# A triangular inverse whose 64-row block is transposed by VectorE instead of TensorE, in a one-core decoder layer

## The chip, the cores and the metric

The kernel runs on one core of one Trainium2 chip, in one launch. A core has five engines that run their own instruction streams and wait for each other on semaphores: TensorE (PE in the profile; PEld is its weight load), VectorE (DVE), ScalarE (ACT), GpSimd (POOL) and SyncE (SP), which here only issues DMAs. The metric is the device time of the launch in microseconds; the median of three runs before the change is 2998.03 us (2996.6 to 2998.27).

## The reference

One layer of a decoder over 2048 tokens of width 1024, in fp32: a gated DeltaNet mixer with 8 heads and a 4-head attention to a memory of 256 rows run side by side, their heads are concatenated and projected, then follow a layer norm, a squared-ReLU MLP of width 4096 and a second layer norm.

```python
proj = x @ w_in                              # q, k, v, z, a, b and the memory's queries
q, k, v = silu(causal_conv4(qkv)); q, k = l2_normalize(q), l2_normalize(k)
a_mat = eye + strict_lower(k_beta @ k.T * decay)     # per head and chunk
u = triangular_solve(a_mat, v_beta); w = triangular_solve(a_mat, k_beta * exp(gc))
# scan over chunks: v_new = u - w @ S; o = q_decay @ S + attn @ v_new; S = S * decay + k_decay.T @ v_new
m = memory_attention(mq, mem_k, mem_v)
x = layer_norm(ALPHA * x + concat(o, m) @ w_out)
x = layer_norm(ALPHA * x + square(relu(x @ w_ff1)) @ w_ff2)
```

## The kernel before, in words

The 2048 tokens are worked on in four blocks of 512. In each block the kernel projects head by head (`dense`, line 673), prepares the head's decay matrices and inverts its triangular matrices (`gdn_a`, 818, which calls `invert`, 732), carries the state through the block's four chunks of 128 tokens (`gdn_b`, 869), does the memory attention and the output projection, and then the MLP. Large products are done as three fp32r matmuls on a high and a low part of each operand: ScalarE casts the high part and VectorE subtracts it to get the low part (`split`). Weights come as 128x1024 tiles `wraw` and are split into `whl`.

`invert` is called 32 times, once for each head and block, for four 128x128 unit lower triangular matrices together (the chunks, `c` in `range(NC)`). It builds the inverse from small blocks up. Blocks of 16 are solved on VectorE. Then each doubling, to 32, 64 and 128, takes two small TensorE products of the same form: `pq`, the off-diagonal block of `L` times a known inverse block, which ScalarE copies to `Q`, and `pp`, another known inverse block times `Q`, which goes with a minus sign into the result. The result `Y` is kept transposed, since the next products want it as weights. The left factor of `pp` is needed the other way round: `X32` for the step to 64 (two VectorE copies out of `Z`, the 32-blocks that VectorE has transposed), and `X64` for the step to 128. Before the change `X64` is made by TensorE: four 64x64 transposes `px` of `Y`'s first 64 rows and columns (line 799), and one VectorE copy from PSUM to SBUF (line 802). All these small products are in plain fp32, which takes two passes for a matmul; a transpose takes one.

The MLP's second product is done in four groups of seven block products (`ff_seven`, 991; the table `SEVEN`, 987). Products 1 to 4 of the table take sums of weight blocks. Those sums are made in the first block by VectorE from `wq` tiles (`keep_sums`, 971), written to DRAM (`tsc`) and read back as `wraw`; the other products read `w_ff2` itself.

The order of the work is not the order of the code. All operations go through a recorder, which gives each a cost and then places them by a list schedule (`cost`, 184, and `issue`, 220): an engine that is free takes the ready operation that comes first in the code, with fixed delays between engines and a limited number of buffers for each tag. The outcome is one fixed order for each engine, and each engine works through its order strictly, waiting where an operand is late. So an edit in one place moves instructions on every engine after it.

Every recorded instruction shows line 320 in the profile; groups are told apart by the names of their tiles.

Of the kernel before, what the change touches and what calls it, by code (L numbers as in the profile page):

```python
# [14 lines left out]
P = 128  # L15
# [321 lines left out]
def hybrid_layer(  # L337
# [31 lines left out]
    cst = ctx.enter_context(tc.tile_pool(name="cst", bufs=1))  # L369
    wp = ctx.enter_context(tc.tile_pool(name="wp", bufs=1))  # L370
    tp = ctx.enter_context(tc.tile_pool(name="tp", bufs=1))
    pad = ctx.enter_context(tc.tile_pool(name="pad", bufs=1))
    nc.vector.memset(pad.tile([P, 112], F32, name="shift"), 0.0)
    sp = ctx.enter_context(tc.tile_pool(name="sp", bufs=1))
    sm = ctx.enter_context(tc.tile_pool(name="sm", bufs=1))
    ps = ctx.enter_context(tc.tile_pool(name="ps", bufs=1, space=bass.MemoryType.PSUM))
# [296 lines left out]
    def dense(b, h, T, G, w0=None):  # L673
        res = {}
        for nm, o in (("q", QO), ("k", KO), ("v", VO), ("z", ZO)):
            w = w0 if w0 and nm == "q" else load_in(b, o // P + h)
            a = bank("a" + nm, "acc")
            project(a, w, T)
            c = slot("c" + nm, "d")
            th = slot("th", "th")  # L680
            if nm == "z":
                nc.scalar.activation(th, a, AF.Tanh, scale=0.5)
                nc.vector.scalar_tensor_tensor(out=c, in0=th, scalar=1.0, in1=a, op0=ALU.add, op1=ALU.mult)
            else:
                gi = o // P + h
                raw = rec.buf(tp, (P, TB + 3), F32, "raw", 2, "raw")
                nc.scalar.copy(out=raw[:, 3:], in_=a)
                nc.gpsimd.tensor_copy(raw[:, 0:3], halo[:, gi].part(gi))
                if b < NB - 1:
                    nc.gpsimd.tensor_copy(halo[:, gi].part(gi), raw[:, TB:TB + 3])  # L690
                nc.scalar.activation(c, a, AF.Copy, scale=cw[:, 72 + gi:73 + gi])
                for j in range(3):
                    nc.vector.scalar_tensor_tensor(out=c, in0=raw[:, j:j + TB], scalar=cw[:, j * 24 + gi:j * 24 + gi + 1],
                                                   in1=c, op0=ALU.mult, op1=ALU.add)
                nc.scalar.activation(th, c, AF.Tanh, scale=0.5)
                nc.vector.scalar_tensor_tensor(out=c, in0=th, scalar=1.0, in1=c, op0=ALU.add, op1=ALU.mult)
            res[nm] = c
            if nm in "qk":
                if "kq" not in res:
                    res["kq"] = [rec.buf(tp, (P, 2, TB), F32R, "kq%d" % u, 1, "kq") for u in range(2)]  # L700
                i = "kq".index(nm)
                split(c, res["kq"][0][:, i].part(i), res["kq"][1][:, i].part(i), KQE)
        par = "ga%d" % (h % 2)
        ss = small("ss", [P, 2 * NC])
        kd = res["kd"] = slot("kd", "s%d" % (h % 2))
        for n, nm in enumerate("kq"):
            pt = bank("pt" + nm, par)
            for c in range(NC):
                nc.tensor.transpose(pt[:, c * P:(c + 1) * P], res[nm][:, c * P:(c + 1) * P], ident)
            for c in range(NC):  # L710
                j = small("j" + nm, [P, P], 1)
                nc.scalar.activation(j, pt[:, c * P:(c + 1) * P], AF.Square,
                                     accum_out=ss[:, n * NC + c:n * NC + c + 1])
            if nm == "k":
                for c in range(NC):
                    nc.scalar.activation(kd[:, c * P:(c + 1) * P], pt[:, c * P:(c + 1) * P], AF.Copy,
                                         scale=G["ekd"][:, h, c:c + 1])
        nc.gpsimd.tensor_scalar_add(ss, ss, 4 * RMS_EPS)
        rk = small("rk", [P, NC])
        nc.gpsimd.tensor_tensor(out=rk, in0=ss[:, :NC], in1=mhalf, op=ALU.pow)  # L720
        res["e4"] = small("e4", [P, NC], 4)
        nc.gpsimd.tensor_scalar_mul(res["e4"], ss[:, NC:], P * RMS_EPS)
        res["vbs"] = small("vbs", [P, NC])
        nc.gpsimd.tensor_tensor(out=res["vbs"], in0=G["betah"][:, h], in1=rk, op=ALU.mult)
        bh = res["bh"] = small("bh", [P, NC])
        nc.gpsimd.tensor_tensor(out=bh, in0=G["beta"][:, h], in1=rk, op=ALU.mult)
        nc.gpsimd.tensor_tensor(out=bh, in0=bh, in1=rk, op=ALU.mult)
        res["nbe"] = small("nbe", [P, NC], 4)
        nc.gpsimd.tensor_tensor(out=res["nbe"], in0=bh, in1=G["neg"][:, h], op=ALU.mult)
        return res  # L730

    def invert(L, par):
# [47 lines left out]
        nc.vector.transpose(Z.rearrange("p c f -> p (c f)"), ZT.rearrange("p c f -> p (c f)"))  # L780
        for p in range(2):
            nc.vector.tensor_copy(X32[32 * p:32 * p + 32, :, 32 * p:32 * p + 32], Z[64 * p:64 * p + 32])
        for r in quads:
            nc.scalar.copy(out=Y3[r, :, r], in_=ZT[r])
        pq = bank("pq", "ga%d" % par)[:64, :P].rearrange("p (c f) -> p c f", c=NC)
        for c in range(NC):
            nc.tensor.matmul(pq[:, c], L32[:, c], ZT[:, c], start=True, stop=True)
        nc.scalar.copy(out=Q[:64, :, :32], in_=pq)
        pp = bank("pp", "ga%d" % par)[:64, :P].rearrange("p (c f) -> p c f", c=NC)
        for c in range(NC):  # L790
            nc.tensor.matmul(pp[:, c], X32[:, c], Q[:, c, :32], start=True, stop=True)
        for p in range(2):
            nc.vector.tensor_scalar_mul(Y3[64 * p:64 * p + 32, :, 64 * p + 32:64 * p + 64],
                                        pp[32 * p:32 * p + 32], -1.0)

        pq = bank("pq", "ga%d" % par)[:64, :2 * P].rearrange("p (c f) -> p c f", c=NC)
        for c in range(NC):
            nc.tensor.matmul(pq[:, c], L[:, c, :64], Y3[:, c, 64:], start=True, stop=True)
        px = bank("px", "ga%d" % par)[:64, :2 * P].rearrange("p (c f) -> p c f", c=NC)
        for c in range(NC):  # L800
            nc.tensor.transpose(px[:, c], Y3[:64, c, :64], ident[:64, :64])
        nc.vector.tensor_copy(X64[:64], px)
        nc.scalar.copy(out=Q[:64], in_=pq)
        pp = bank("pp", "ga%d" % par)[:64, :2 * P].rearrange("p (c f) -> p c f", c=NC)
        for c in range(NC):
# [165 lines left out]
    def keep_sums(u, j):  # L971

        if j == 0:
            B = [t[:, n * TB:(n + 1) * TB].part(n) for t in (tok_tile("wq"), tok_tile("wq")) for n in range(2)]
        else:
            B = [rec.buf(tp, (P, TB + 3), F32, "raw", 2, "wq")[:, :TB] for _ in range(2)]
            kq = rec.buf(tp, (P, 2, TB), F32, "kq1", 1, "wq")
            B += [kq[:, n].part(n) for n in range(2)]
        for n in range(4):
            nc.sync.dma_start(out=B[n], in_=w_ff2[u + 2 * (n // 2), n % 2][:, j * TB:(j + 1) * TB])  # L980
        for i, o, x, y in ((1, 0, 1, 0), (3, 1, 3, 1), (2, 3, 3, 0), (4, 2, 2, 3)):
            nc.vector.tensor_tensor(out=B[o], in0=B[x], in1=B[y], op=ALU.subtract)
            nc.sync.dma_start(out=tsc[u, i][:, j * TB:(j + 1) * TB].part(j), in_=B[o])
# [7 lines left out]
    def ff_seven(b, ff1_tiles, relu2, add, norm2):  # L991
        Q = 2 * P
        for g in range(NS):
# [45 lines left out]
            if last:  # L1039
                gb = load_bcast(ln2_g, "l2g"), load_bcast(ln2_b, "l2b")  # L1040
            banks = {}
            for n, (xn, wn, bn, on, (th, nh)) in enumerate(SEVEN):
                if not on:
                    banks[bn] = [bank("af2", ("ga%d" % t) if bn == "A" else "pb") for t in range(2)]
                w = [None, None]
# [223 lines left out]
```

## Time and profile before

| what | value |
|---|---|
| median of three runs | 2998.03 us |
| the profiled execution, by its own time | 2999.08 us |
| its span from first to last instruction | 2997.4 us |
| PE busy | 2945.4 us (98%), 15300 matmul passes |
| DVE busy | 2168.6 us (72%) |
| ACT busy | 1520.3 us (51%) |
| POOL busy | 332.4 us (11%) |
| mean granted TensorE clock | 0.995 of full speed |

A matmul's recorded duration runs into the next one's, since matmuls are pipelined: a 128x512 product shows about 0.39 us while the next one starts 0.23 us after it. What a matmul takes of the span is therefore read from start to start in the timeline. In a timeline row, the columns are the start, the duration from the first to the last instruction merged into the row, the engine, the operation with its tiles, the shape and the count; a bracket holds the idle time just before it and what ended it.

### The profile page before, as it was taken

What the parts mean: (1) busy time and instruction counts of PE and PEld (TensorE: products, weight loads), DVE (VectorE), ACT (ScalarE), POOL (GpSimd) and SP (SyncE); (2) the same over time, 40 slices, a digit from 0 to 9 for tenths busy, and PEclk for the clock granted to TensorE, in tenths of its full rate; (3) what the DMA queues carried; (4) which work ended last, traced back from release to release, by engine and by line L of the source; (5) the groups of instructions that cost most, each with busy time, mean ns of one, the idle gap of its engine ahead of it and who ended that gap; (6) DMA issues with size and microseconds to landing.
All of it is one profiled execution on the core that took longest, in us unless ns stands there. A gap on an engine that the chain in (4) does not pass through costs nothing.

```text
span 2997.4 us, 43880 instructions
## 1 busy us (share of the span) xinstructions
PE 2945.4 (98%) x15300; PEld 2428.1 (81%) x15300; DVE 2168.6 (72%) x5537; ACT 1520.3 (51%) x3582; POOL 332.4 (11%) x808
## 2 busy tenths in 40 slices
PE   7999999999999999999999999999999999999998
PEld 6888788888788878888878887888878888788886
DVE  6898977666777787655577887665667787675667
ACT  5676534544355562544445665344554556444443
POOL 1222100000112211000012221000001222000000
PEclk9999999999999999999999999999999999999999
DMA  6765566656733223444473332244446332324443
GB/s 231 253 218 180 196 209 224 200 183 192 268 142 132 106 89 102 145 137 133 151 268 130 121 119 92 87 152 144 145 159 250 126 134 96 99 88 146 143 147 134
DMA packets 127709, 469.85 MB, mean 157 GB/s; under 512 B 14464, under 2 KB 16896, under 8 KB 109056
## 3 DMA queue, kind: packets, MB, share of 16 engines
q1 hardware_dynamic: 126912, 467.00, 46.2%
q8 instruction: 120, 1.97, 0.3%
q14 instruction: 101, 0.83, 0.1%
q10 hardware_dynamic: 576, 0.06, 0.0%
HBM read 402.97 MB, written 64.03 MB: 156 GB/s over the span
## 4 chain that ended last, share of the span: by engine, by line
PE 88%; DVE 8%; ACT 2%; issue 1%; DMA 1%; POOL 0%; POOLq 0%; ACTq 0%; DVEq 0%; SPq 0%
PE af L320 42%; PE ao L320 8%; PE aq L320 6%; PE ak L320 5%; PE az L320 5%; PE av L320 4%; PE amq L320 3%; PE pc L320 3%; PE pp L320 2%; PE pq L320 2%; PE po L320 2%; PE pkq L320 1%; DVE y L320 1%; PE sps L320 1%; DVE ck L320 1%
## 5 line engine op out<-in xcount | busy, mean ns | idle before, releaser
L320 DVE TENSOR_TENSOR whl<-wraw,whl 128x1024 fp32r<-128x1024 f32 (+1 forms) x446 | 538.7, 1216 | 392.8 <-ACT whl L320 386.1
L320 PE MATMUL af<-Thi,whl 128*128 128x512 f32 (+1 forms) x2304 | 655.9, 369 | 6.9 <-DVE whl L320 4.0
L320 ACT CAST whl<-wraw 128x1024 fp32r<-128x1024 f32 (+1 forms) x446 | 466.1, 1045 | 381.8 <-PE af L320 169.0
L320 PEld LDWEIGHTS af<-Thi,whl 128*128 128x128 f32 x2304 | 421.7, 191 | 78.5 <-DVE whl L320 4.8
L320 PE MATMUL af<-whl,xh 128*128 128x512 f32 x1536 | 476.4, 391 | 3.6 <-DVE whl L320 3.6
L320 PE MATMUL af<-Tlo,whl 128*128 128x512 f32 (+1 forms) x1152 | 424.8, 369 | 0.0
L320 PE MATMUL af<-whl,xl 128*128 128x512 f32 x896 | 347.3, 390 | 0.0
L320 PEld LDWEIGHTS af<-whl,xh 128*128 128x128 f32 x1536 | 288.6, 188 | 68.6 <-DVE whl L320 6.7
L320 PE MATMUL ao<-whl,ch 128*128 128x512 f32 x768 | 249.4, 399 | 0.5 <-DVE y L320 0.5
L320 PEld LDWEIGHTS af<-Tlo,whl 128*128 128x128 f32 x1152 | 220.4, 191 | 34.8
L320 ACT ACTIVATE rl<-af 128x512 f32<-128x512 f32 x128 | 76.5, 598 | 271.0 <-PE af L320 269.0
L320 DVE SCALAR_TENSOR_TENSOR y<-y,af 128x512 f32<-128x512 f32 x224 | 151.3, 684 | 84.1 <-PE af L320 82.9
L320 PEld LDWEIGHTS af<-whl,xl 128*128 128x128 f32 x896 | 168.5, 188 | 35.5
L320 POOL TENSOR_SCALAR ve<-mv 128x1 f32<-128x1 f32 x34 | 23.3, 684 | 1528.8 <-DVE mv L320 1528.8
L320 PE MATMUL aq<-Thi,whl 128*128 128x512 f32 x512 | 181.6, 414 | 7.5 <-ACT Thi L320 7.5
L320 PE MATMUL av<-Thi,whl 128*128 128x512 f32 x512 | 173.0, 402 | 0.0
L320 PE MATMUL ak<-Thi,whl 128*128 128x512 f32 x512 | 172.9, 401 | 0.0
L320 PE MATMUL az<-Thi,whl 128*128 128x512 f32 x512 | 170.2, 400 | 0.0
L320 PEld LDWEIGHTS ao<-whl,ch 128*128 128x128 f32 x768 | 142.6, 188 | 27.0 <-DVE y L320 0.7
L320 PE MATMUL ao<-whl,cl 128*128 128x512 f32 x384 | 153.5, 400 | 0.0
L320 PEld LDWEIGHTS aq<-Thi,whl 128*128 128x128 f32 x512 | 94.3, 192 | 21.5 <-ACT Thi L320 7.5
L320 PEld LDWEIGHTS az<-Thi,whl 128*128 128x128 f32 x512 | 95.9, 190 | 18.8 <-DVE whl L320 0.5
(252 smaller groups left out, 5756.3 us busy)
## 6 DMA issues: line engine op xcount, KB each, us to landing
wraw<-in_w_ff_dram SPq DMA_DIRECT2D x224, 512.0 KB, 4.0
whl<-wsc SPq DMA_DIRECT2D x108, 1024.0 KB, 4.8
wraw<-tsc SPq DMA_DIRECT2D x128, 512.0 KB, 3.3
wsc<-whl SPq DMA_DIRECT2D x36, 1024.0 KB, 4.9
wraw<-in_w_out_dram SPq DMA_DIRECT2D x48, 512.0 KB, 4.1
wraw<-in_w_in_dram SPq DMA_DIRECT2D x35, 512.0 KB, 5.8
wq<-in_w_ff_dram SPq DMA_DIRECT2D x64, 256.0 KB, 4.3
tsc<-wq SPq DMA_DIRECT2D x64, 256.0 KB, 3.3
```

Source lines behind the costliest of these rows:

```text
L320: o.fn(*[res(a) for a in o.args], **{k: res(v) for k, v in o.kw.items()})
```

## The change

Three things are changed.

`X64` is now put together from pieces that exist earlier. Its two diagonal 32-blocks are copied by GpSimd out of `Z` (two new copies of 32x128 per call). Its off-diagonal block is the result `pp` of the step to 64, transposed: VectorE transposes the 32 first rows of that PSUM bank in blocks of 32x32 into the buffer of `Lq`, whose contents are no longer needed by then, and writes it with a minus sign into `X64`. The four TensorE transposes and VectorE's copy of `px` are gone. The upper right block of `X64` stays zero from the memset at the start.

The 448-byte tile `shift`, which only moved what is allocated behind it, is gone, and each of the two `raw` buffers is 224 bytes longer. So the second `raw` buffer lies 224 bytes further, the two `kq` buffers 448 bytes further, and all that follows lies where it was.

In the first group of the first block, the product `A12*B21`, which reads `w_ff2` itself, comes second instead of sixth.

```diff
-    pad = ctx.enter_context(tc.tile_pool(name="pad", bufs=1))
-    nc.vector.memset(pad.tile([P, 112], F32, name="shift"), 0.0)
...
-                raw = rec.buf(tp, (P, TB + 3), F32, "raw", 2, "raw")
-                nc.scalar.copy(out=raw[:, 3:], in_=a)
+                raw = rec.buf(tp, (P, TB + 3 + 56), F32, "raw", 2, "raw")
+                nc.scalar.copy(out=raw[:, 3:TB + 3], in_=a)
...
         for p in range(2):
             nc.vector.tensor_copy(X32[32 * p:32 * p + 32, :, 32 * p:32 * p + 32], Z[64 * p:64 * p + 32])
+            nc.gpsimd.tensor_copy(X64[32 * p:32 * p + 32, :, 32 * p:32 * p + 32], Z[32 * p:32 * p + 32])
...
-        pp = bank("pp", "ga%d" % par)[:64, :P].rearrange("p (c f) -> p c f", c=NC)
+        p32 = bank("pp", "ga%d" % par)
+        pp = p32[:64, :P].rearrange("p (c f) -> p c f", c=NC)
         for c in range(NC):
             nc.tensor.matmul(pp[:, c], X32[:, c], Q[:, c, :32], start=True, stop=True)
+        t32 = Lq[:32].rearrange("p f c -> p (f c)")
+        nc.vector.transpose(t32, p32[:32, :P])
         for p in range(2):
             nc.vector.tensor_scalar_mul(Y3[64 * p:64 * p + 32, :, 64 * p + 32:64 * p + 64],
                                         pp[32 * p:32 * p + 32], -1.0)
+        nc.vector.tensor_scalar_mul(X64[32:64, :, :32], t32.rearrange("p (c f) -> p c f", c=NC), -1.0)
...
-        px = bank("px", "ga%d" % par)[:64, :2 * P].rearrange("p (c f) -> p c f", c=NC)
-        for c in range(NC):
-            nc.tensor.transpose(px[:, c], Y3[:64, c, :64], ident[:64, :64])
-        nc.vector.tensor_copy(X64[:64], px)
...
-            B = [rec.buf(tp, (P, TB + 3), F32, "raw", 2, "wq")[:, :TB] for _ in range(2)]
+            B = [rec.buf(tp, (P, TB + 3 + 56), F32, "raw", 2, "wq")[:, :TB] for _ in range(2)]
...
-            for n, (xn, wn, bn, on, (th, nh)) in enumerate(SEVEN):
+            order = [0, 5, 1, 2, 3, 4, 6] if b == 0 and g == 0 else range(7)
+            for n, (xn, wn, bn, on, (th, nh)) in enumerate(SEVEN[i] for i in order):
```

Since the schedule is made anew, instructions move on every engine. Three places matter below.

On PE, the first inversion of the first block, from the product `pp` of the step to 64 (`X_162`, afterwards `X_157`, is the tile X32; `X_160` is the new kernel's X64; `ak` and `av` are the projections that fill the time). Before:

```order
L320 MATMUL pp<-Q,X_162 64x32 x4
L320 MATMUL ak<-Thi,whl 128x512 x2
L320 MATMUL ak<-Tlo,whl 128x512
L320 MATMUL ak<-Thi,whl 128x512
L320 MATMUL av<-Thi,whl 128x512
L320 MATMUL pq<-Y,dl 64x64 x4
L320 MATMUL av<-Tlo,whl 128x512
L320 MATMUL av<-Thi,whl 128x512 x2
L320 MATMUL av<-Tlo,whl 128x512
L320 MATMUL av<-Thi,whl 128x512
L320 MATMUL px<-ident,Y 64x64 x4
L320 MATMUL av<-Thi,whl 128x512
```

The same place in the changed kernel:

```order
L320 MATMUL pp<-Q,X_157 64x32 x4
L320 MATMUL ak<-Thi,whl 128x512 x2
L320 MATMUL ak<-Tlo,whl 128x512
L320 MATMUL ak<-Thi,whl 128x512
L320 MATMUL av<-Thi,whl 128x512
L320 MATMUL av<-Tlo,whl 128x512
L320 MATMUL pq<-Y,dl 64x64 x4
L320 MATMUL av<-Thi,whl 128x512 x2
L320 MATMUL av<-Tlo,whl 128x512
L320 MATMUL av<-Thi,whl 128x512
L320 MATMUL pp<-Q,X_160 64x64 x4
```

The transposes `px` are gone, `pq` stands behind six large matmuls instead of five, and the last `pp` follows `pq` after four large matmuls.

On DVE, the same inversion, between the product `pp` of the step to 64 and the last write to `Y` before `pq` (the `Lq<-dl` copies belong to the next head). Before:

```order
L320 SCALAR_TENSOR_TENSOR cq<-th,cq 128x512
L320 TENSOR_SCALAR Y<-pp 32x4x32
L320 COPY Lq<-dl 32x4x32
L320 TENSOR_SCALAR Y<-pp 32x4x32
L320 COPY Lq<-dl 32x4x32
```

And in the changed kernel:

```order
L320 SCALAR_TENSOR_TENSOR cq<-th,cq 128x512
L320 STREAM_TRANSPOSE Lq<-pp 32x128
L320 TENSOR_SCALAR Y<-pp 32x4x32
L320 TENSOR_SCALAR X_160<-Lq 32x4x32
L320 COPY Lq<-dl 32x4x32
L320 TENSOR_SCALAR Y<-pp 32x4x32
```

Two operations more, the transpose and the write to X64, stand ahead of the second write to `Y`.

On SP, where the first group of the first block's MLP begins (`wraw<-in_w_ff_dram` loads weights of either MLP product, `tsc<-wq` writes the weight sums, `wraw<-tsc` reads them back). Before:

```order
L320 DMA wraw<-in_w_ff_dram 128x1024
L320 DMA wq<-in_w_ff_dram 128x512 x5
L320 DMA wraw<-in_w_ff_dram 128x1024
L320 DMA wraw<-tsc 128x1024
L320 DMA tsc<-wq 128x512 x2
L320 DMA wq<-in_w_ff_dram 128x512
L320 DMA tsc<-wq 128x512 x4
L320 DMA wraw<-tsc 128x1024
```

And in the changed kernel:

```order
L320 DMA wraw<-in_w_ff_dram 128x1024
L320 DMA tsc<-wq 128x512 x2
L320 DMA wq<-in_w_ff_dram 128x512
L320 DMA wraw<-in_w_ff_dram 128x1024
L320 DMA tsc<-wq 128x512 x2
L320 DMA wq<-in_w_ff_dram 128x512
L320 DMA tsc<-wq 128x512 x2
L320 DMA wraw<-tsc 128x1024
```

The first read-back of a sum now stands behind the loads of one more product and behind more of the writes.

## The prediction

> **What bounds the kernel now.** I read the page's engine shares and its chain of waits first.
>
> ```profile
> PE 2945.4 (98%) x15300; PEld 2428.1 (81%) x15300; DVE 2168.6 (72%) x5537; ACT 1520.3 (51%) x3582; POOL 332.4 (11%) x808
> PE 88%; DVE 8%; ACT 2%; issue 1%; DMA 1%; POOL 0%; POOLq 0%; ACTq 0%; DVEq 0%; SPq 0%
> ```
>
> PE is busy for 98% of the span and makes 88% of the chain that ended last. Next I read who PE waited for; the columns are total us, times and the longest wait.
>
> ```profile
> PE af L320 <- DVE whl L320: 7.6, 10, 1.5
> PE aq L320 <- ACT Thi L320: 7.5, 1, 7.5
> PE ptk L320 <- DVE ck L320: 5.7, 4, 2.0
> ...
> PE pp L320 <- ACT Q L320: 1.6, 6, 0.3
> ```
>
> Nothing larger stands in that view. PE hardly waits, and nowhere for `X64`, the tile that the change makes in another way. So the time is the sum of PE's steps, and the question is what the change does to that sum, and whether it makes PE wait where it now does not.
>
> **The transposes.** Here is PE's timeline at the first inversion, the one whose order is shown above.
>
> ```profile
> 113.81 0.65 PE L320 MATMUL pp<-Q,X 128*64 128x32 f32 x8
> 114.39 0.73 PE L320 MATMUL ak<-Thi,whl 128*128 128x512 f32 x2
> ...
> 115.42 0.40 PE L320 MATMUL av<-Thi,whl 128*128 128x512 f32 x1
> 115.75 0.68 PE L320 MATMUL pq<-Y,dl 128*64 128x64 f32 x8
> ...
> 116.69 0.63 PE L320 MATMUL av<-Thi,whl 128*128 128x512 f32 x2
> 117.16 0.40 PE L320 MATMUL av<-Tlo,whl 128*128 128x512 f32 x1
> 117.39 0.39 PE L320 MATMUL av<-Thi,whl 128*128 128x512 f32 x1
> 117.71 0.41 PE L320 MATMUL px<-ident,Y 64*64 64x64 f32 x4
> 118.05 0.50 PE L320 MATMUL av<-Thi,whl 128*128 128x512 f32 x1
> 118.39 0.40 PE L320 MATMUL av<-Tlo,whl 128*128 128x512 f32 x1
> ```
>
> Large matmuls follow each other in 0.23 us (two from 116.69 to 117.16, one to 117.39). Around `px`, one large matmul, the four transposes and one more large matmul take from 117.39 to 118.39, 1.00 us, where the two alone would take 0.46. The four transposes thus cost 0.54 us: their own 0.34, and 0.1 each for going to the small form and back (0.32 and 0.34 instead of 0.23). There are 128 transposes, so 32 such visits:
>
> ```profile
> L320 PE MATMUL px<-ident,Y 64*64 64x64 f32 x128 | 14.3, 224 | 0.0
> L320 DVE COPY X<-px 64x256 f32<-64x256 f32 x32 | 13.3, 416 | 14.8 <-PE px L320 14.4
> L320 DVE TENSOR_SCALAR Y<-pp 32x128 f32<-32x128 f32 x64 | 18.0, 281 | 9.8 <-PE pp L320 8.7
> L320 DVE COPY X<-Z 32x128 f32<-32x128 f32 x64 | 14.2, 221 | 0.9
> L320 DVE STREAM_TRANSPOSE Z<-ZT 128x128 f32<-128x128 f32 x32 | 9.8, 306 | 0.2
> L320 POOL COPY L<-dl 32x128 f32<-32x128 f32 x64 | 31.2, 487 | 24.7 <-PE pq L320 14.9 <-DVE Bc L320 7.5
> ```
>
> 32 x 0.54 = 17.3 us. In some inversions other small products split the four and the cost is higher, so I take **-18 us**, with 14 (the busy time alone) and 20 as the ends.
>
> **The rest of PE's order.** The new schedule puts other small groups elsewhere: some now stand beside each other, others alone. A group that is set among large matmuls costs the two 0.1 us just read. I added up, for both orders, the usual step of each matmul behind its two predecessors as the trace has it, and the changed order comes out about 5 us shorter beyond the transposes, but part of that is short waits that the trace has in such places. I take **-3 us**, between -5 and +2, the loss being some ten more visits at 0.2.
>
> **What VectorE and GpSimd get.** Per inversion, VectorE loses the 416 ns copy of `px` and gets a transpose out of PSUM and a 32x128 write. The trace has no transpose out of PSUM. The same kind from SBUF takes 306 ns for 128x128. Out of PSUM a 32x128 write takes 281 ns, against 221 for the copy from SBUF, so reading PSUM adds at most 60: the transpose is between 306 and 366 ns, and I take 0.35 us, since its PSUM source puts it nearer to the upper end; the lower bound is already too high if 32 partitions are quicker. The write to `X64` reads SBUF and is nearest to the 221. Net, VectorE gets 0.15 us more per inversion, 5 us in all. It is hidden under PE as long as VectorE is not the bound, and it comes nearest to that in the first block:
>
> ```profile
> 130.00:190.00 60.00, 59.87 (x368) 50.02 (x366) 55.21 (x192) 45.06 (x143) 20.00 (x45) 1.00 0.63 213
> ```
>
> VectorE is busy for 55.21 of 60 us here, and PE for 59.87. If that cover is gone, the price is eight inversions at 0.15, 1.2 us. GpSimd gets two copies of 487 ns, 31 us in all on an engine that works 11% of the span. They need `Z` and are used two TensorE steps later; behind them on GpSimd wait the next head's `raw` copies and `LB` pieces. I cost them at nothing; the price without cover is the same half microsecond per head on VectorE's convolutions, not on PE.
>
> **The new place to wait.** The chain from `pp` (step to 64) to `pq` (step to 128) gets longer, since the transpose and the write to `X64` stand ahead of the second write to `Y`. VectorE at the same inversion:
>
> ```profile
> 114.50 0.28 DVE L320 TENSOR_SCALAR Y<-pp 32x128 f32<-32x128 f32 x1
> 114.71 0.26 DVE L320 COPY Lq<-dl 32x128 f32<-32x128 f32 x1
> 114.98 0.28 DVE L320 TENSOR_SCALAR Y<-pp 32x128 f32<-32x128 f32 x1
> ```
>
> The second write ends at 115.26 and `pq` starts at 115.75, 0.49 us later. Such small operations follow each other in 0.21 to 0.27 us, so two more put the end at about 115.75; `pq` moves by one large matmul to 115.98. What is left is 0.23 us, still enough here. Where VectorE is late, it is not:
>
> ```profile
> 190.73 0.27 DVE L320 TENSOR_SCALAR Y<-pp 32x128 f32<-32x128 f32 x1
> ...
> 191.21 0.28 DVE L320 TENSOR_SCALAR Y<-pp 32x128 f32<-32x128 f32 x1
> ```
>
> ```profile
> 189.82 0.62 PE L320 MATMUL pp<-Q,X 128*64 128x32 f32 x8
> ...
> 191.73 0.68 PE L320 MATMUL pq<-Y,dl 128*64 128x64 f32 x8
> ```
>
> VectorE comes to `Y` 0.9 us after the first `pp`, not 0.7, ends at 191.49, and would end at about 191.95, just when the moved `pq` is due (191.96): a wait of 0.1 to 0.2 us for the semaphore. Ten of the 32 inversions in the trace have VectorE this late or later, and in the changed order three have only two or three large matmuls between `pq` and the last `pp`, where `Q`'s copy must fit. The bounds are nothing and 0.4 us for each of 32, 13 us; I take **+3 us**, 0.3 for each of the ten. Behind a late `pq` the whole of PE is queued, and then all that waits for PE.
>
> On the other side, the last `pp` no longer waits behind `px` and its copy, and the inversion ends a microsecond earlier. Nothing that PE waits for in the list above comes out of `Y`, so I give this nothing.
>
> **The product order.** Where the first group of the MLP begins, PE waits three times for weights:
>
> ```profile
> 513.89 0.51 PE L320 MATMUL af<-whl,xh 128*128 128x512 f32 x1 [0.29 <-DVE whl L320]
> 521.09 0.50 PE L320 MATMUL af<-whl,xh 128*128 128x512 f32 x1 [1.47 <-DVE whl L320]
> 527.21 0.50 PE L320 MATMUL af<-whl,xh 128*128 128x512 f32 x1 [0.29 <-DVE whl L320]
> ```
>
> ```profile
> 515.80 1.05 ACT L320 CAST whl<-wraw 128x1024 fp32r<-128x1024 f32 x1 [4.88 <-DMA wraw<-tsc]
> ```
>
> They are 2.05 us, and the cast behind them had waited 4.88 us for a sum read back from DRAM. The product moved ahead is 24 matmuls, 24 x 0.23 = 5.5 us of work that needs no sum. That covers the 4.88, and on SP the loads of its weights come ahead of the first read-back. I take **-2 us**, between 0 (the next sum is late instead) and -2.05.
>
> **The moved buffers.** Whether the address of `kq` matters can be read from tiles that already lie at the two kinds of places: `hq` shares `kq`'s buffer, and `xh` lies in the 2 KB tiles behind it, whose offset within 2 KB `kq` takes over.
>
> ```profile
> L320 DVE TENSOR_TENSOR xl<-ss,xh 128x512 fp32r<-128x512 f32 x96 | 62.4, 688 | 2.5 <-ACT xh L320 2.5
> L320 DVE TENSOR_TENSOR xl<-ss,hq 128x512 fp32r<-128x512 f32 x32 | 20.7, 687 | 0.0
> L320 PE MATMUL af<-whl,xh 128*128 128x512 f32 x1536 | 476.4, 391 | 3.6 <-DVE whl L320 3.6
> L320 PE MATMUL af<-whl,hq 128*128 128x512 f32 x256 | 80.1, 394 | 0.0
> ```
>
> 688 against 687 ns and 391 against 394: nothing, within 3 ns of 400, and at 1% of the matmuls on `kq` less than 1 us either way. Taking out the memset of `shift` is 0.2 us at a time when PE waits for `Thi` anyway.
>
> **The sum**: -18 - 3 + 3 - 2 = **-20 us**. Against the profiled execution's own 2999.08 us (its span of 2997.4 and 1.7 around it) that gives 2979; the runs' median is 1 us lower, so **2978 us**.
>
> **The rivals.** *The wait takes the transposes' place.* If VectorE is late at every inversion by 0.65 us, 32 x 0.65 = 21 us go into `pq`, against the 23 that the other terms gain: 2998 - 23 + 21 = 2996, no change that can be told. For it speaks that the slack of 0.49 and 0.24 us is no longer than two small operations; against it that the order puts a large matmul between as well.
>
> *PE's clock halves.* The trace shows what two close waits can do:
>
> ```profile
> 449.50:453.40 3.90, 1.64 (x12) 1.22 (x11) 3.90 (x7) 1.49 (x2) 0.70 (x1) 0.99 0.00 0
> 453.40:456.80 3.40, 3.40 (x19) 3.40 (x18) 3.40 (x6) 0.00 (x0) 1.31 (x2) 0.51 0.88 284
> ```
>
> PE was idle for 2.26 of 3.9 us, and the granted clock in the 3.4 us behind was 0.51, which costs 1.7 us. If `pq` and the last `pp` both wait for about 1.1 us in one inversion, that inversion loses 2.3 + 1.7 = 4.0 us. Six such use up the gain; if all eight of the first block, where VectorE is fullest, and four later ones are hit, the time is 2998 - 23 + 48 = 3023, and from six on the change is slower. Against it: the single 1.47 us above was not followed by a slow stretch, and waits of a microsecond at `pq` would need VectorE four small operations behind its order. The Trainium skill, in "TensorE: Matmul & The Clock Gate", Part 1, says that the clock falls after an idle window of about 3.4 us; by that rule no such wait could bring it down and this rival would have no chance. The rows show a fall after less, in two pieces, so it keeps a small one.
>
> *More than the sum.* All ends on the good side, -20 - 5 - 2 and no new wait: 2971, and 2966 if the shorter inversion also frees some of the 15 us that PE waits for `whl`, `ck` and `Q`. For it: the waits are there. Against: they come from weights and convolutions.
>
> *VectorE as the bound.* 5 us at most if nothing hides them, 2983; inside the range.
>
> **How the numbers follow.** The sum as forecast, between 2970 and 2990: 0.76. More than the sum: 0.11. No change, 2992 to 2999: 0.08. Slower, by the clock or by waits of over 0.9 us at most inversions: 0.05. The range goes from 2965 (all good ends) to 2991 (-14 + 2 + 6 + 0 = -6, with half of the wait's upper end, since not all 32 are late; 2992, less one), and leaves about 0.15 outside. About 0.2%, 6 us, is what a measurement of this kernel can tell from no change. Faster by more than that: 0.87; within it: 0.08; slower: 0.05.
>
> **What would show it.** No `px` rows, and PE's busy time lower by some 20 us, as much as the span. In PE's waits, new rows `pq` waiting for DVE `Y` and `pp` for ACT `Q` should come to about 3 us; 15 or more would mean that the chain took the gain. The transpose from PSUM should show 0.31 to 0.37 us; over 0.6 and the waits grow. The wait of 1.47 us in the first group should be gone. `pkq` and the `kq` writes should keep their durations. The prediction is wrong if PE's idle time grows by 10 us or more, or if the granted clock has new stretches of 0.5 in the head phase.

## The result: 2980.26 us, and the profile after

Four runs of the changed kernel took 2977.27, 2978.14, 2982.86 and 2982.37 us, median 2980.26, against 2998.15 before: a ratio of 0.9941, with a 95% interval of 0.9924 to 0.9958. The forecast was 2978 us. The profiled run is the first of the four, 2977.27 us with a span of 2975.6.

The engine shares and the shares of the chain of waits, of the kernel after:

```profile
PE 2920.6 (98%) x15172; PEld 2416.7 (81%) x15172; DVE 2172.7 (73%) x5568; ACT 1523.1 (51%) x3582; POOL 340.5 (11%) x872
PE 90%; DVE 6%; ACT 2%; issue 1%; DMA 1%; POOL 0%; POOLq 0%; ACTq 0%; DVEq 0%; SPq 0%
```

PE lost 128 matmul passes and 24.8 us of busy time, and it still bounds the kernel. VectorE got 4.1 us. Who PE waited for, after (us in total, times, longest):

```profile
PE af L320 <- DVE whl L320: 11.3, 10, 2.9
PE aq L320 <- ACT Thi L320: 7.4, 1, 7.4
...
PE pp L320 <- ACT Q L320: 2.0, 6, 0.4
PE af L320 <- ACT whl L320: 1.6, 3, 0.6
...
PE pp L320 <- DVE X L320: 0.9, 3, 0.4
```

No row says that PE waited for `Y` at `pq`, the wait that the forecast had priced at 3 us. The last row shown is new and was not forecast: in the first block, three products `pp` of the step to 64 wait for VectorE's copies into `X32` (it shares the name `X` with `X64`), 0.9 us in all. The wait of `af` for weights that VectorE ends rose from 7.6 to 11.3 us; with the part that ScalarE ends, 2.9 before, it rose from 10.5 to 12.9. It had been expected to fall by 2.

PE's timeline at the first inversion of the kernel after, from the product `pp` of the step to 64 to that of the step to 128:

```profile
113.36 0.65 PE L320 MATMUL pp<-Q,X 128*64 128x32 f32 x8
...
115.21 0.40 PE L320 MATMUL av<-Tlo,whl 128*128 128x512 f32 x1
115.54 0.68 PE L320 MATMUL pq<-Y,dl 128*64 128x64 f32 x8
116.14 0.73 PE L320 MATMUL av<-Thi,whl 128*128 128x512 f32 x2
116.71 0.40 PE L320 MATMUL av<-Tlo,whl 128*128 128x512 f32 x1
116.95 0.40 PE L320 MATMUL av<-Thi,whl 128*128 128x512 f32 x1
117.27 0.68 PE L320 MATMUL pp<-Q,X 128*64 128x64 f32 x8
```

`px` is gone, and nothing is idle in its place. The new operations by their groups (busy us, mean ns of one, idle before them):

```profile
L320 POOL COPY X<-Z 32x128 f32<-32x128 f32 x64 | 21.8, 340 | 71.0 <-DVE Z L320 66.9 <-DVE Xc L320 2.4
L320 DVE TENSOR_SCALAR Y<-pp 32x128 f32<-32x128 f32 x64 | 16.9, 264 | 0.8
L320 DVE STREAM_TRANSPOSE Lq<-pp 32x128 f32<-32x128 f32 x32 | 9.7, 302 | 12.2 <-PE pp L320 12.0
L320 DVE TENSOR_SCALAR X<-Lq 32x128 f32<-32x128 f32 x32 | 7.0, 217 | 0.7
```

The transpose out of PSUM takes 302 ns on 32 partitions, no more than the 306 ns of the one from SBUF on 128.

**The clock.** The profiles also show pieces of 3.41 us in which the granted clock is 0.5; where PE is fed throughout, such a piece costs about half its length, 1.7 us. Both profiles have one of 6.8 us at about 33 us and a last one at the end of the span, in which no matmul runs. Between them the kernel before has four: at the start of the first MLP (the one the prediction showed) and of each later one. The kernel after has two: at the start of the first MLP, and one at 223.7 us in the head phase, the stretch of a block from its projections to its MLP. Here is the start of the second MLP, before (window; its length; busy time and count of PE, PEld, DVE, ACT, POOL; granted clock; DMA share; GB/s), with PE's two waits in it:

```profile
1187.20:1190.60 3.40, 1.85 (x14) 1.44 (x13) 3.40 (x6) 0.99 (x2) 0.71 (x1) 1.00 0.00 0
1190.60:1194.00 3.40, 3.40 (x19) 3.40 (x18) 3.40 (x6) 0.00 (x0) 1.30 (x2) 0.50 0.83 265
```

```profile
1188.24 0.39 PE L320 MATMUL af<-Thi,whl 128*128 128x256 f32 x1 [0.55 <-ACT whl L320]
1189.74 0.51 PE L320 MATMUL af<-Thi,whl 128*128 128x256 f32 x2 [1.00 <-DVE whl L320]
```

After, the very same waits stand there, and no slow piece behind them:

```profile
1179.50:1182.90 3.40, 2.85 (x23) 2.50 (x22) 3.34 (x7) 2.12 (x3) 0.00 (x0) 1.00 0.13 51
1182.90:1186.30 3.40, 2.40 (x20) 2.34 (x20) 3.40 (x5) 0.00 (x0) 2.01 (x2) 1.00 0.40 93
1186.30:1189.70 3.40, 3.40 (x31) 3.40 (x30) 3.40 (x6) 1.17 (x2) 0.00 (x0) 1.00 0.58 220
```

```profile
1182.46 0.39 PE L320 MATMUL af<-Thi,whl 128*128 128x256 f32 x1 [0.55 <-ACT whl L320]
1183.96 0.50 PE L320 MATMUL af<-Thi,whl 128*128 128x256 f32 x2 [1.00 <-DVE whl L320]
```

Before, both waits lie in one window (1.55 us idle). After, the border of two windows lies between them (0.55 and 1.00). So a part of the profiled pair's 21.8 us is not the change. To take it out I read each stage from its first matmul to that of the next (a head phase from its first `ak`, an MLP from its first `af`), and take off half of what ran at half clock. By this, in us against the kernel before (four head phases, four MLPs):

| kernel | heads | sum | MLPs | sum | both |
|---|---|---|---|---|---|
| after | -4.6 -4.3 -4.5 -4.7 | -18.1 | +1.6 -0.6 -0.5 -0.6 | -0.1 | -18.2 |
| new block alone | -4.0 -4.5 -4.6 -5.0 | -18.1 | +0.5 +0.2 +1.2 +0.2 | +2.1 | -16.0 |
| order alone | -0.3 0.0 +0.4 -0.3 | -0.2 | +0.3 0.0 +0.2 0.0 | +0.5 | +0.3 |
| buffers alone | +1.0 +0.2 -0.2 -0.1 | +0.9 | -0.7 -0.6 -0.8 -0.9 | -3.0 | -2.1 |
| all but the order | -3.7 -4.4 -4.7 -4.8 | -17.6 | +0.4 -0.6 -0.5 -0.6 | -1.3 | -18.9 |
| no transposes | -4.1 -4.1 -4.3 -4.3 | -16.8 | -0.4 +0.1 0.0 +0.2 | -0.1 | -16.9 |
| transposes twice | -0.6 +2.3 +2.0 +2.0 | +5.7 | +2.4 +0.6 +0.2 +0.2 | +3.4 | +9.1 |
| Y later by half | -1.8 -2.6 -2.8 -3.0 | -10.2 | +1.7 -0.8 -0.6 -0.6 | -0.3 | -10.5 |

The change is worth about 18 us at full clock. The other 3 to 4 us of the profiled pair are the clock: by half their length, the pieces between the first and the last cost 6.8 us before and 3.4 after.

The table is good to a microsecond or two, and its first column is the weakest. The first 41 us of PE's work hold the same 151 matmuls in the same order in every kernel, ahead of any inversion, and yet they differ by the same reckoning: by -0.3 us after, +0.6 in the new block alone, -0.3 with the order alone, +0.7 with the buffers alone, +0.5 in all but the order, +1.7 without transposes, 0.0 with them twice and +0.1 with `Y` later. (In the kernel without transposes the piece near 33 us is half as long and yet this part took as long as before, so a piece does not cost half its length where PE also waits.) Without these 41 us the last column reads -17.9, -16.6, +0.6, -2.8, -19.4, -18.6, +9.1 and -10.6.

### The profile page after: what moved, and what is told of

Read it like the earlier page. It is cut to its first block, busy times and chain, and to the rows that moved or that the text cites. A ratio compares the mean times of both kernels' runs of the same rounds, so it can differ in the third digit from the quotient of the medians.

```text
span 2975.6 us, 43770 instructions
## 1 busy us (share of the span) xinstructions
PE 2920.6 (98%) x15172; PEld 2416.7 (81%) x15172; DVE 2172.7 (73%) x5568; ACT 1523.1 (51%) x3582; POOL 340.5 (11%) x872
## 4 chain that ended last, share of the span: by engine, by line
PE 90%; DVE 6%; ACT 2%; issue 1%; DMA 1%; POOL 0%; POOLq 0%; ACTq 0%; DVEq 0%; SPq 0%
PE af L320 43%; PE ao L320 8%; PE az L320 6%; PE aq L320 6%; PE ak L320 5%; PE av L320 5%; PE amq L320 3%; PE pc L320 3%; PE pp L320 2%; PE pq L320 2%; PE po L320 2%; PE pkq L320 1%; DVE y L320 1%; PE sps L320 1%; DVE whl L320 1%
```

## The experiments

**1. The change in its parts.** Three kernels do one part alone, and one does all but the product order. Here the parts are not shown again; each is one of the diff's three. Each ratio here and below is to runs of the kernel before on the same chip; the experiments used three chips, so their medians compare less well than their ratios.

The new block alone:

> The kernel before with the new way to make X64 alone; the buffers and the product order stay. Theory A (the transposes and PE's order behind them are all of the gain): -18 -3 and at most +3 for the new place to wait, so 2977 to 2983 us, -15 to -21 against before, PE busy lower by 20 to 25 us, the four head phases each shorter by 4 to 5 us (the first by about 3), and no PE wait for Y at pq. Rival B (the moved buffers or the product order carry a part of it): a gain of under 12 us here. Since the sums' read-backs stay where they were, the MLP's three waits for weights in the first group should stay near 0.29, 1.47 and 0.29 us (about 2 us in all).

Measured: 2982.29 us (2978.75 to 2984.27), ratio 0.9944 [0.9931, 0.9958]. Theory A's time and its head phases are right: -4.0, -4.5, -4.6 and -5.0, where about -3 was expected of the first. Its profile has the three waits in the first group at 0.54, 0.29 and 1.47 us.

The order alone:

> The kernel before with the product A12*B21 second in the first group, and nothing else changed. The prediction's term: -2 us (2996), the wait of 1.47 us gone. Theory from the two traces: the writes of the sums stand on SP behind weight loads that wait for a free buffer, so the read-back comes no earlier, and the first group's waits for weights sum to 2 to 4 us as they do after the change; the time is within 2 us of before, 2998 to 3000.

Measured: 2997.86 us (2996.82 to 3000.04), ratio 0.9999 [0.9990, 1.0007]. The prediction's -2 us is not there. In its first group PE waits twice:

```profile
514.48 0.50 PE L320 MATMUL af<-whl,xh 128*128 128x512 f32 x1 [1.45 <-DVE whl L320]
521.70 0.49 PE L320 MATMUL af<-whl,xh 128*128 128x512 f32 x1 [1.45 <-DVE whl L320]
```

That is 2.90 us, where it was 2.05. The wait has been moved and has grown.

The buffers alone:

> The kernel before with the tile shift taken out and the raw buffers longer, nothing else. The prediction's term: nothing, less than 1 us either way, 2997 to 2999, with the matmuls and the writes on kq as long as before (pkq 294 ns, the TensorE products of kq within 3 ns). Rival: the new addresses of raw and kq matter for VectorE's convolutions or for TensorE's operands: then a row on raw, cq or kq shows over 5 ns of difference, and the time differs by over 3 us.

Measured: 2995.39 us (2992.55 to 2998.72), ratio 0.9989 [0.9980, 0.9998]. Neither theory had it. The rows on `kq` and the convolutions are as before, but the row on `hq`, whose difference the prediction had counted as nothing, is not. First the kernel with the moved buffers, then the new block alone, where `hq` lies as before:

```profile
L320 PE MATMUL af<-whl,hq 128*128 128x512 f32 x256 | 78.8, 389 | 0.0
```

```profile
L320 PE MATMUL af<-whl,hq 128*128 128x512 f32 x256 | 80.1, 394 | 0.0
```

Read from start to start, matmuls with `hq` took up to 237 ns before and mostly 226 or 227 after the move; with the matmuls beside them that is about 0.05 us for each of 16 groups in an MLP, 0.8 us, and the MLPs of the table are shorter by 0.6 to 0.9. All kernels with the moved buffers show it, none of the others does.

All but the order:

> The changed kernel with the table's own product order. If the order is worth what the prediction said, this is 2 us slower than the changed kernel; if the traces are read rightly (the waits for weights in the first group rose from 2.05 to 3.64 us, and the first MLP came out 1.6 us longer), this is 1 to 2 us faster than the changed kernel, 2976 to 2981, and the first group's waits come back to about 2 us. On the clock: the number of 3.41 us stretches at half clock (three here or six, each 1.7 us) may shift the time by up to 5 us either way, so the stretches in its profile are to be counted before the two are compared.

Measured: 2976.80 us (2975.36 to 2980.88), ratio 0.9929 [0.9917, 0.9942]. Its profile has one half-clock piece between the first and the last, at the first MLP. The waits in the first group are 0.54, 0.30 and 1.47 us, 2.31 in all against 3.64 in the changed kernel, and the first MLP is shorter by 1.2 us. The product order is no gain; in this setting it costs 1 to 1.5 us. The 3.5 us between the two medians hold the clock as well.

**2. What a visit to the transposes costs.** Between the two settings of `rec.hidden`, here and below, the planner counts an operation as nothing.

```diff
         for c in range(NC):
             nc.tensor.transpose(px[:, c], Y3[:64, c, :64], ident[:64, :64])
+        rec.hidden = True
+        for c in range(NC):
+            nc.tensor.transpose(px[:, c], Y3[:64, c, :64], ident[:64, :64])
+        rec.hidden = False
```

> The kernel before, with each group of four 64x64 transposes done twice in a row; the planner is told that the second four cost nothing, so the order is as before. The prediction priced a visit at 0.54 us: 0.34 for the four and 0.1 each for going to the small form and back. If that split is right, four more without another change of form cost 32 x 0.23 to 0.34, so 7 to 11 us more than before, spread over the four head phases at about 2 us each. Rival: the visit costs what the transposes themselves take and the two changes of form are nothing, so four more cost the whole 0.54, 17 us.

Measured: 3003.16 us (3001.57 to 3006.47), ratio 1.0017 [1.0008, 1.0026]. At full clock it is 9.1 us longer. That sum is not the price of the transposes alone. The planner counted them as nothing, but the order did not stay: in each head phase many other matmuls stand elsewhere, and the first head phase came out 0.6 us shorter in spite of its longer visits; and the first MLP has 2.4 of the 9.1, by waits for weights (seven, of 6.3 us in all, where the kernel before has five of 4.3). The price is read at the visit itself. Here is the first inversion, the place that the prediction showed:

```profile
117.35 0.39 PE L322 MATMUL av<-Thi,whl 128*128 128x512 f32 x1
117.67 0.63 PE L322 MATMUL px<-ident,Y 64*64 64x64 f32 x8
118.23 0.50 PE L322 MATMUL av<-Thi,whl 128*128 128x512 f32 x1
118.57 0.40 PE L322 MATMUL av<-Tlo,whl 128*128 128x512 f32 x1
```

From the large matmul ahead of `px` to the second one behind, this takes 1.22 us, against 1.00 before. From the first `px` to the next matmul it is 0.56 us in all 32 visits here, and 0.34 in all 26 visits of the kernel before that other products do not split. So four more right behind the first cost 0.22 us, 7.0 for 32 visits and the lower end of what was forecast, and not 0.54. The other 0.32 us of a visit come once, however many transposes it holds; the prediction had 0.2 of this kind, for going to the small form and back.

The visit itself stays at 0.54: in the kernel before, 23 of the 32 visits stand between large matmuls, and all of them take 0.99 to 1.01 us there. For the nine others (six split in two, three beside another small product) 0.45 to 0.65 each is my estimate, from their own steps with and without the changes of form. Together the transposes took 16 to 18 us.

**3. The transposes left out, with nothing in their place.**

```diff
-        px = bank("px", "ga%d" % par)[:64, :2 * P].rearrange("p (c f) -> p c f", c=NC)
-        for c in range(NC):
-            nc.tensor.transpose(px[:, c], Y3[:64, c, :64], ident[:64, :64])
-        nc.vector.tensor_copy(X64[:64], px)
```

> The kernel before without the transposes and without VectorE's copy of them, and nothing in their place: X64 stays zero, so the 64-row off-diagonal block of the inverse is left out as zero (its products are still computed). The prediction's theory: the transposes are worth 18 us and the rest of PE's order 3, so -18 to -21 here. Rival: the chain from pp to pq in the changed kernel took a part of the gain; then this kernel, which has no new work in that chain, is faster than the new block alone by 3 us or more. If the chain is free, it is within 2 us of it.

Measured: 2978.08 us (2976.24 to 2978.86), ratio 0.9932 [0.9918, 0.9946]; -16.9 us at full clock, against -16.0 for the new block alone, or -18.6 against -16.6 without the first 41 us. By this the whole of the new work on VectorE and GpSimd costs PE 1 to 2 us, which is within the 2 us of a free chain and short of the rival's 3. It is no clean price, since PE's order in the head phases differs between the two kernels. Of the waits that can be named, the new block alone has two for `X32`, 0.7 us, and this kernel none. That the chain took a large part of the gain is out.

**4. How much room the new chain has.** Two more VectorE reads of the bank stand ahead of the transpose:

```diff
+        rec.hidden = True
+        for _ in range(2):
+            nc.vector.reduce_max(out=small("dum", [P, 1], 4)[:32], in_=p32[:32, :P], axis=AX.X)
+        rec.hidden = False
         nc.vector.transpose(t32, p32[:32, :P])
```

> The changed kernel with two more VectorE reads of the pp bank (32x128, about 0.25 us each) ahead of the transpose, which the planner takes as free, so that the order stays and Y comes about 0.5 us later at every inversion. The trace of the changed kernel has 0.15 to 0.72 us from the last write of Y to pq, with 0.15 as the least that the semaphore needs. If the chain is that close, PE waits at pq for Y by the sum over the inversions of what exceeds the slack, 8 to 11 us in all, and the time rises by as much. Rival: VectorE has more room than this (the write is early where it matters), then PE waits less than 3 us and the time stays within 3 us.

Measured: 2986.73 us (2985.17 to 2991.49), ratio 0.9964 [0.9950, 0.9978]. PE's order is that of the changed kernel. At full clock it is 7.7 us longer, all of it in the head phases. Its list of PE's waits has a new row:

```profile
PE pq L322 <- DVE Y L322: 4.6, 17, 0.3
```

The row shows 4.6 us where the time shows 7.7. The rest is hidden by the way a matmul is recorded: its end lies 0.16 us behind the start of the next one, so that much of a wait counts as busy. From start to start, the matmul ahead of `pq` took 444 to 740 ns in 26 of the 32 inversions, where 320 is usual, 7.5 us more in all. So Y is needed within half a microsecond almost everywhere. In the changed kernel itself the shortest distance from the last write of `Y` to `pq` is 0.15 us, in the third inversion, first on VectorE, then on PE:

```profile
187.69 0.30 DVE L320 STREAM_TRANSPOSE Lq<-pp 32x128 f32<-32x128 f32 x1
187.93 0.24 DVE L320 TENSOR_SCALAR Y<-pp 32x128 f32<-32x128 f32 x1
188.18 0.22 DVE L320 TENSOR_SCALAR X<-Lq 32x128 f32<-32x128 f32 x1
188.41 0.28 DVE L320 COPY Lq<-dl 32x128 f32<-32x128 f32 x1
188.70 0.28 DVE L320 TENSOR_SCALAR Y<-pp 32x128 f32<-32x128 f32 x1
```

```profile
188.79 0.39 PE L320 MATMUL av<-Thi,whl 128*128 128x512 f32 x1
189.13 0.65 PE L320 MATMUL pq<-Y,dl 128*64 128x64 f32 x8
```

The step from 188.79 to 189.13 is 0.03 us over the usual 0.32. It is the only one of the 32 that waited at all. The next ones had 0.01 to 0.05 us to spare.

**5. Why the product order brought nothing.** In the changed kernel, ScalarE's cast for the first wait, and VectorE's rows behind it:

```profile
507.06 1.05 ACT L320 CAST whl<-wraw 128x1024 fp32r<-128x1024 f32 x1 [3.33 <-DMA wraw<-tsc]
```

```profile
506.00 3.22 DVE L320 TENSOR_TENSOR wq<-wq 128x512 f32<-128x512 f32 x5
509.13 1.22 DVE L320 TENSOR_TENSOR whl<-wraw,whl 128x1024 fp32r<-128x1024 f32 x1
```

and SP's queue, where the time is what an entry took to get through:

```profile
497.33 6.25 SPq L320 DMA_DIRECT2D wraw<-tsc  x2
503.83 5.73 SPq L320 DMA_DIRECT2D tsc<-wq  x7
510.38 10.89 SPq L320 DMA_DIRECT2D wraw<-tsc  x4
```

My theory was that the writes of the sums are held up on SP behind loads that wait for a buffer. The experiment gives them ScalarE's queue:

```diff
-            nc.sync.dma_start(out=tsc[u, i][:, j * TB:(j + 1) * TB].part(j), in_=B[o])
+            nc.scalar.dma_start(out=tsc[u, i][:, j * TB:(j + 1) * TB].part(j), in_=B[o])
```

> The changed kernel with the writes of the weight sums to DRAM issued from ScalarE's DMA queue instead of SP's. Theory: in the changed kernel the read-backs come late because the writes stand on SP behind weight loads that wait for a free wraw buffer (5.7 and 10.9 us in its trace), so moving the product by 5.5 us of work brought nothing. On their own queue the sums are in DRAM earlier and the three waits for weights in the first group (1.88, 0.30 and 1.46 us) fall to 1 us or less in all; the first MLP is 2 to 3 us shorter, the time 2976 to 2979. Rival: the read-backs wait on SP themselves for a free wraw buffer, whatever the writes do; then the waits in the first group stay at 3 us or more and the time is within 1.5 us of the changed kernel at the same number of half-clock stretches.

Measured: 2982.65 us (2976.34 to 2985.96), ratio 0.9945 [0.9930, 0.9960], with five waits in the first group, of 0.17, 0.53, 0.21, 1.03 and 1.46 us, 3.4 in all. At full clock it equals the changed kernel. The rival's numbers fit, and the theory does not stand. ScalarE now waits for the sums themselves:

```profile
509.06 1.05 ACT L323 CAST whl<-wraw 128x1024 fp32r<-128x1024 f32 x1 [5.67 <-DVE wq L323]
```

The last sums leave VectorE only between 506 and 514 us here, and at 503 to 509 in the changed kernel. Whether they or the free `wraw` buffers end the wait is not settled by this: the experiment also put a wait into ScalarE's own order.

**6. The half-clock pieces.** The time of a run goes with its mean granted clock: the kernel with all but the order took 2975.36 us at 0.997 and 2980.88 at 0.995. So I tested the cause of these pieces. In two kernels, ten matmuls that use operands already there fill most of the two waits at the start of the second, third and fourth MLP; the bank that they write is started anew right after:

```diff
+                    if b and halves and t0 == 0 and i == 1:
+                        rec.hidden = True
+                        for _ in range(10):
+                            nc.tensor.matmul(a[:, :256], wa[0][0][0][0], T1[0][:, 0, :256].part(0, 1), start=True, stop=True)
+                        rec.hidden = False
                     project(a[:, t0:t0 + n], w, T1, n, t0)
```

In the changed kernel without the product order:

> The changed kernel with the table's own product order and, at the start of the second, third and fourth MLP, ten 128x256 matmuls (0.12 us each) of operands that are there already, into the bank that the next product starts anew, just where PE waits 0.55 and 1.00 us for weights. They only fill time that PE waits through. Theory: the half-clock stretch of 3.41 us follows where PE was idle for about 1.55 us within one piece of a fixed 3.41 us grid, and the two waits reach that when they fall into one piece. Filled, they leave at most 0.5 us: no half-clock stretch at these three places in any run, so the time is at or below the fastest of the kernel without the filling (2975 to 2976), where that one varies by up to 5 us, the mean falls by 1 to 3 us. Rival: the stretches come from something else (the change of tile shapes there, the chip's load): then they stay as often as before, and the time is the same or longer by up to 3 us.

Measured: 2975.06 us (2974.77 to 2977.72), ratio 0.9925 [0.9912, 0.9938]. In the kernel before:

> The kernel before with the same thirty filling matmuls at the start of the second, third and fourth MLP. Theory of the clock: the three half-clock stretches that its profile shows there (1.7 us each) are gone in every run, and nothing else changes: 2994 to 2996, 2 to 5 us less than before, with PE's waits for weights in those places down from 1.55 to about 0.4 us. Rival (the stretches do not depend on PE's idle time): time and stretches as before.

Measured: 2994.01 us (2992.94 to 2999.11), ratio 0.9987 [0.9978, 0.9997]. Neither profile has a half-clock piece at these MLPs, and the idle time there is down from 1.55 to 0.62 us. Of the first one, the filled wait:

```profile
1178.80 1.60 PE L322 MATMUL af<-Thi,whl 128*128 128x256 f32 x12
...
1181.62 0.50 PE L322 MATMUL af<-Thi,whl 128*128 128x256 f32 x2 [0.62 <-DVE whl L322]
```

More work on PE made the kernel before faster; the interval says 1 to 7 us. The runs are not all as low as forecast: in the kernel before two of ten lie above 2996 (2997.52 and 2999.11), and without the product order two of five lie above 2976. The profile of the run of 2997.52 us has a half-clock piece of 6.8 us elsewhere, in a head phase. The filled kernel's median without the product order is the lowest of all here; against the same kernel without the filling, 2976.80 and a ratio of 0.9929, its interval does not separate it.

## Why the prediction was right, and where it was not

**The bound.** PE, before and after; VectorE's 4.1 us more (5 forecast) are hidden but for the 1 to 2 us of experiment 3 at most. The 0.9 us of waits for `X32` fall in the first block, where the prediction saw VectorE nearest to being the bound and priced a lost cover at 1.2 us; that the new work causes these waits is not shown.

**Transposes -18, rest of the order -3.** Together they are what the head phases lost: -18.1 in the changed kernel and in the new block alone (-17.8 and -18.6 without the first 41 us). So their sum was about 3 us too large. The visits of experiment 2 put the transposes at 16 to 18, so the first term stands and the 0.54 us read at one place is right for most of the others. What was mis-sized is the rest of the order: by this difference it brought some 0 to 2 us, not 3, with the 0.9 us of new waits for `X32` in it as a loss. Which groups the term had wrong beyond these is not shown.

**VectorE and GpSimd.** 0.302 us for the transpose instead of 0.35, below the lower bound of 0.306; 0.217 for the write, where 0.221 stood; 340 ns for a GpSimd copy, where 487 did. Nearly all hidden, as forecast.

**The new wait, +3.** This term was mis-sized: 0.03 us in all. The mechanism is right, since half a microsecond more on VectorE makes 26 of 32 inversions wait. The step that failed is the count of ten. It took how late VectorE comes to `Y` behind the first `pp`, and not how far `Y` lies from `pq`. By that distance only four inversions of the profile before are close, with 0.15 to 0.31 us; the next has 0.46. With 0.46 us of new work and 0.23 for the moved matmul, as the prediction had them, and the 0.15 us that `pq` needs in the slowed kernel's 26 waits, those four would have waited some 0.6 us in all by my estimate. The new order did better still: in the third inversion `Y` ended 0.235 us before `pq` in the old order, and in the new one 0.15 us, just enough. With -21 for the other two terms too large by 3 and this one too large by 3, the head phases came out as summed, -18, by two errors that cancel. That is luck.

**Product order, -2.** This step failed: between 0 and +1.5. The prediction counted 5.5 us of work that needs no sum against a cast that waited 4.88 us, and took what waits for the sums as fixed in time. It is not. In the profile after, the cast behind the moved product still waits for its read-back, VectorE has five sums ahead of the rest of the same weights, and the wait of 1.47 us that was to go is there with 1.46.

**Buffers, 0.** This step failed too, by -2 to -3 us. The prediction looked at the right rows, 391 against 394 ns for `hq`, and called the difference nothing; it counted "1% of the matmuls on `kq`", and not the 256 on `hq` and the ones behind them. This error and that of the product order are some 2 to 3 us each and have opposite signs, so they cancel as well, again by luck.

**The sum.** -20 forecast, -18.2 at full clock; with the clock, 21.8 in the profiled pair and 18 in the medians.

**The rivals.** The wait in the transposes' place is out (experiments 3 and 4). The clock did not turn against the change by the way that the rival gave: the new `pq` does not wait. But one of the prediction's signs of being wrong is there, a new half-clock piece in the head phase, at 223.7 us. Set beside the kernel with all but the order, whose PE has the same order up to there and no such piece, it costs 1.4 us. Kernels without the new block have such pieces too, so it is not shown to come from the change. And the rival had the right thing in view. The Trainium skill, in "TensorE: Matmul & The Clock Gate", Part 1, says that the clock is set by a free-running window of 3413 ns; the grid here is 3.41 us and its offset differs from run to run, which agrees. It also says that the clock falls after an idle window. By that these waits could not bring it down, and the runs disagree: a window with 1.55 us of idle time was enough. The same waits cost 1.7 us or nothing by where the grid lies. Three MLPs with such a piece make 5 us, as much as lies between the runs of 2977 and of 2983; that these runs differ by it is likely, but only the first of them has a profile.

## What to carry to other kernels

Where one engine is busy for 98% of the time, price an edit by what it takes off that engine from start to start, with the change of form on both sides; and then see whether the new chain still meets the schedule's distance, because here it did so by a few hundredths of a microsecond. That distance is from the last write of an operand to the instruction that reads it, and not from the work that came before. A load or product moved earlier is only worth its length if what the next step waits for stays where it was. Before 5 us of difference are put down to an edit, count the half-clock pieces in both profiles; and short waits of PE that lie close together can be worth filling, even with matmuls whose result is thrown away: one of the two kernels here got faster by it, and for the other the runs do not tell.

## What the runs showed of the hardware that was not expected

- **The clock's threshold.** In the ten profiles without filling there are 30 starts of a second, third or fourth MLP, all with the waits of 0.55 and 1.00 us. In 13 of them both lay within one window of the grid (1.55 to 1.57 us idle), and all 13 were followed by a half-clock piece. In the other 17 the border cut them (0.95 to 1.54 us in the fuller window), and none was. This holds for these places only: windows in the first group of the MLP's second product with 1.63 and 1.88 us, of a single wait, were not followed by one, nor were two near the end of the kernel, with 1.73 (the buffers alone) and 1.92 us (the kernel before, filled). So the idle time of a window is not the whole rule.
- **Half-clock pieces in the head phase.** The changed kernel has one at 223.7 us, behind a window with 0.46 us idle:

```profile
220.30:223.70 3.40, 2.94 (x23) 2.33 (x22) 3.36 (x10) 1.80 (x6) 1.21 (x2) 1.00 0.00 0
223.70:227.10 3.40, 3.40 (x14) 2.39 (x14) 3.34 (x15) 2.74 (x7) 1.86 (x7) 0.51 0.17 70
```

 That window also holds sixteen small matmuls of 128x16. Kernels without the new block have such pieces too (the kernel before with filling at 1736.7 us, the moved buffers alone at 2335.0). That light work counts like idle time would explain them, but no run tests it.
- **Where an operand lies.** 448 bytes made 5 ns of difference in the mean, and up to 10, to a matmul with `hq` (232 against 227 ns from start to start), on PE's time and with no wait in the profile. Why is not shown.
- **A change of form on PE.** A visit of four 64x64 transposes among 128x512 matmuls costs 0.54 us, and four more in the same visit 0.22.
- **A wait can be busy time.** Up to 0.16 us of each wait of PE behind a large matmul appears as busy, so the list of waits showed 4.6 of 7.5 us.
